# Native float32 products for the first six weight slots of layer 0, and the rotary tables computed after the first GLA

## The chip, the cores and the metric

The kernel runs on one core of a Trainium2 chip. The metric is device time in microseconds (us) of one execution. The core has a matrix engine (TensorE, PE in the profile; its weight loads are listed as PEld), a vector engine (VectorE, DVE), a scalar engine (ScalarE, ACT), a general engine (GpSimd, POOL) and a queue engine (SyncE, SP) that mostly issues transfers from device memory. Each engine runs its own fixed list of instructions in order, and waits on semaphores for the others.

## What is computed

Two layers of a streaming-encoder trunk on 256 tokens of width 1024, everything in float32. Each layer normalises its input, shifts and scales it by values computed from a conditioning vector c (adaLN), multiplies it by one wide input matrix, feeds three token mixers (attention with rotary keys, RWKV-7, gated linear attention or GLA), and merges them.

```python
cos, sin = _rope_tables(positions)
c_act = jax.nn.silu(c)
for l in range(DEPTH):                                  # 2 layers
    mod = c_act @ ada_w[l] + ada_b[l]                   # 1024 -> 3 x 1024
    shift, scale, gate = jnp.split(mod, 3, axis=-1)
    h = _rms_norm(x, norm_pre[l]) * (1 + scale[:, None, :]) + shift[:, None, :]
    p = h @ w_in[l]
    ...
    o_mla = _mla_branch(m_cq, m_ckv, m_kr, m_z, cos, sin, ...)
    o_rwkv = _rwkv7_branch(r_streams, r_z, ...)
    o_gla = _gla_branch(g_q, g_k, g_v, g_l, g_z, ...)
    merged = (sigmoid(gate_a) * o_mla + sigmoid(gate_b) * o_rwkv + sigmoid(gate_c) * o_gla)
    y = merged @ w_out[l]
    x = x + gate[:, None, :] * _rms_norm(y, norm_post[l])
```

## The kernel before

Activations lie transposed: 128 partitions of features, 8 feature blocks (`KD`), 256 tokens. The input matrix is cut in **slots** of 256 output columns; a slot is two transfers of 512 KB (128x1024 each) and makes one 2x256-column PSUM bank, by 8 blocks x 2 halves = 16 products of 128x128 weights by 128x256 tokens.

A product of full float32 precision is made of three products in the type float32r: weights and activations are each split into a rounded part `hi` and a rest `lo`, and `hi*hhi + hi*hlo + lo*hhi` is summed. For the weights this is done in `weights` (L333 to L347): the transfer into `wr`, the copy to `hi` on ACT (L344), the subtraction to `lo` on DVE or POOL (L345). The activations are split by `split` (L388 to L392) into `hhi` and `hlo`, once, and kept for the layer. `dense` (L358) and `dense_tok` (L371) run the products. `wr`, `hi` and `lo` rotate through four buffers each.

**The head** of the program, `start` (L268 to L320), makes layer 0's normed input and the first six slots (lora0, rk000, rk001, rr000, rr001, rv000). It loads x (L275), squares it on ACT, sums the squares of each token on PE (`sums`, L144), and takes the root and reciprocal in `rms_row` (L397): reduce, root, reciprocal on 128x2 values, then `to_rows` (L146) and `spread` (L162) turn these into a row and copy it to all partitions by two more products. x is multiplied by it (L285). Then an order string is walked, "WaWaWaWaWaWaaa". A `W` takes up one slot: its loads and splits, and a product of zeros (L315) that opens its bank. An `a` takes up one feature block k: `ada_part` (L254) loads two 512 KB tiles of the adaLN matrix and reduces each with c in one DVE instruction (L263, scalar_tensor_tensor, STT below), `ada_in` (L322) makes shift and scale, ACT applies them (L303), `split` makes `hhi` and `hlo`, and the products of block k with the slots so far follow (`mm`, L288 to L295, products at L293). In four of the six slots POOL makes `lo`. 

`rope_tables` (L172 to L213), 34 POOL instructions on 128x256 tiles and two sines on ACT, stands ahead of `start` in the program.

**Behind the head** come, for layer 0: the rest of the RWKV slots and the GLA gates (`pg`, L800, which reads the 32 KB tile `gw`), GLA's slots gq, gk, gv, `rw_prep` for half of the heads, `rw_chain(0)` (L562), `gla`, `rw_prep` and `rw_chain` for the other half, attention, and the output. In `rw_chain` a matrix `Bb` is loaded, POOL computes a triangular inverse `Xb` in 31 dependent pairs (L607 to `tm`, L610 to `Xb`), the result goes out and back by a transfer (`Xs`), and then a loop over chunks starts with the product `u` (L692).

A planner with its own model of times orders each engine's list at build time; the program text decides only what depends on what, and which pools and rotations a tile uses.

Of the kernel before, what the change touches and what calls it, by code (L numbers as in the profile page):

```python
# [10 lines left out]
F32 = mybir.dt.float32  # L11
# [65 lines left out]
def trunk(  # L77
# [94 lines left out]
    def rope_tables():  # L172
        with tc.tile_pool(name="rope", bufs=1, reuse_waits="tile") as rp:
            posi = rp.tile([P, T], I32, name="posi")
            nc.sync.dma_start(posi, pos.partition_broadcast(P))
            ang = rp.tile([P, T], F32, name="ang")
            G.tensor_copy(ang, posi)
            G.tensor_scalar(ang, ang, ifreq, None, ALU.mult)
            turn = rp.tile([P, T], F32, name="turn")
            pieces, inv2pi = _turn_pieces()  # L180

            def wrap(t):
                r = rp.tile([P, T], F32, tag="wrap", name="wrap", bufs=2)
                G.tensor_scalar(r, t, MAGIC, -MAGIC, ALU.add, ALU.add)
                G.tensor_sub(t, t, r)

            first = True
            for k, hi, lo in pieces:
                m = MAGIC * 2.0 ** k
                n = rp.tile([P, T], F32, tag="n", name="n", bufs=2)  # L190
                G.tensor_scalar(n, ang, m, -m, ALU.add, ALU.add)
                G.tensor_sub(ang, ang, n)
                a = rp.tile([P, T], F32, tag="ta", name="ta", bufs=2)
                G.tensor_scalar(a, n, 2.0 ** -k, hi, ALU.mult, ALU.mult)
                wrap(a)
                b = rp.tile([P, T], F32, tag="tb", name="tb", bufs=2)
# [7 lines left out]
            b = rp.tile([P, T], F32, tag="tb", name="tb2", bufs=2)  # L204
# [62 lines left out]

    def start(L, hl, firsts, order):  # L268
# [2 lines left out]
        hhi, hlo = hl  # L271
        zero = pp.tile([P, 1], F32, name="zero")
        G.memset(zero, 0.0)
        xn = pp.tile([P, KD, T], F32, name="xn0")
        nc.sync.dma_start(xn, xt)  # L275
        ss = ps_m.tile([P, 2, KD], F32, tag="m", name="ss0")
        for s in range(4):
            sq = pp.tile([P, 2, T], F32, tag="sq", name="sq0", bufs=2)
            A.activation(sq, xn[:, 2 * s:2 * s + 2], AF.Square)
            for i in range(2):  # L280
                sums(ss[:, :, 2 * s + i:2 * s + i + 1], sq[:, i], one_b)
        ri = rms_row(pp, ss, 1.0 / D, "0")
# [3 lines left out]
        slots, ks, left = [], [], {}  # L286

        def mm(w, ps, k):  # L288
            left[id(ps)] -= 1
            ws = slice(k * P, (k + 1) * P)  # L290
            for i, (hi, lo) in enumerate(w):
                for j, (wt, at) in enumerate(((hi, hhi), (hi, hlo), (lo, hhi))):
                    PE.matmul(  # L293
                        ps[:, i].rearrange("p (a b) -> p a b", a=2), wt[:, ws], at[:, :, k],
                        start=False, stop=i == 1 and j == 2 and left[id(ps)] == 0)  # L295

        for what in order:
            if what == "a":
                k = len(ks)
                ada_part(L, 0, (k,), pp)  # L300
                ada_in(L, k, k + 1)
                hT = pp.tile([P, T], F32, tag="hT0", name="hT0", bufs=3)
                A.activation(hT, xn[:, k], AF.Identity, scale=L.s1[:, k:k + 1], bias=L.mod[:, k:k + 1])  # L303
                split(hhi[:, :, k], hlo[:, :, k], hT.rearrange("p (a b) -> p a b", a=2))
                ks.append(k)
                for w, ps in slots:
                    mm(w, ps, k)
            else:
                n, src, pool, tag = firsts[len(slots)]
                j = len(slots)  # L310
                w = weights(src, n, pool=None if j < 2 else pp, sub=G if j in (1, 3, 4, 5) else V)
                ps = pool.tile([P, 2, T], F32, tag=tag, name=f"ps_{n}")
                left[id(ps)] = KD
                early[n] = ps
                PE.matmul(  # L315
                    ps.rearrange("p a b -> p (a b)"), zero.broadcast_to([P, P]), zero.broadcast_to([P, 512]),
                    start=True, stop=False)
                slots.append((w, ps))
# [821 lines left out]
    rw = ctx.enter_context(tc.tile_pool(name="rw", bufs=1))  # L1140
    for l in range(DEPTH):
        h = halves_of(hl)
# [14 lines left out]
        with tc.tile_pool(name=f"rc{l}0", bufs=1, reuse_waits="tile") as rc:  # L1157
# [142 lines left out]
```

## Time and profile before

| | us |
| --- | --- |
| timed runs, median of three | 1174.64 (1173.78 to 1175.44) |
| the profiled execution, its own time | 1172.76 |
| its span in the trace | 1171.0 |
| PE busy, share of the span | 1091.8 (93%) |
| PEld / DVE / ACT / POOL busy | 85% / 68% / 49% / 40% |

The profile was taken of one execution; its 1172.76 us lie 1.88 us below the median of the timed runs. PE is busy most of the time, but its busy share is lowest at the start: the tenths of the first three fortieths (29 us each) read 5, 8, 9 in the page's second part, and the granted TensorE clock in the same slices reads 7, 7, 9 tenths of full speed. Times in the trace count from the start of the span. A PE row's duration covers the whole passage of one instruction; back-to-back products overlap, so that the distance between two starts, not the duration, is what one costs.

### The profile page before, as it was taken

How to read it: one execution, taken by the hardware profiler on the slowest of the kernel's cores; microseconds unless marked ns; L12 is line 12 of the kernel's file. 1: busy time of each engine (PE TensorE's matmuls, PEld its weight loads, DVE VectorE, ACT ScalarE, POOL GpSimd, SP SyncE). 2: the span in 40 equal slices, each digit the busy share in tenths (PEclk: the TensorE clock that was granted, in tenths of full speed). 3: DMA queues.
4: the chain of work that ended last, by engine and by line, in shares of the span. 5: the costliest groups of instructions: out<-in, count | busy, mean ns of one | idle time of the engine just before them, and what ended most of it. 6: DMA issues, size and time to landing. Idle time of an engine off the chain costs nothing.

```text
span 1171.0 us, 25069 instructions
## 1 busy us (share of the span) xinstructions
PE 1091.8 (93%) x10293; PEld 997.3 (85%) x10293; DVE 791.7 (68%) x1204; ACT 576.9 (49%) x982; POOL 467.2 (40%) x617
## 2 busy tenths in 40 slices
PE   5899988899999699999989999899999979999997
PEld 3788888798898588899989888889899968789997
DVE  5968955666887666667665694385587666657763
ACT  4357334445456343445556833364383635346452
POOL 7954638425426833203100635541073753311210
PEclk7799998999999899999999999899999989999999
DMA  9665654654466454446654255334434543244761
GB/s 362 211 197 174 164 170 127 193 185 152 130 217 193 145 158 95 131 136 214 224 181 152 89 162 151 113 108 140 143 117 145 181 129 93 86 123 139 247 206 45
DMA packets 70068, 185.15 MB, mean 158 GB/s; under 512 B 24609, under 2 KB 25121, under 8 KB 69825
## 3 DMA queue, kind: packets, MB, share of 16 engines
q1 hardware_dynamic: 48304, 173.37, 47.6%
q10 hardware_dynamic: 21648, 10.18, 3.3%
q8 instruction: 81, 1.33, 0.4%
q14 instruction: 35, 0.28, 0.1%
HBM read 179.32 MB, written 4.20 MB: 157 GB/s over the span
## 4 chain that ended last, share of the span: by engine, by line
PE 60%; POOL 15%; DMA 10%; DVE 6%; ACT 4%; issue 4%; ACTq 1%; SPq 0%; DVEq 0%; POOLq 0%
PE ps_gt L358 10%; PE ps_wo L358 9%; POOL tm L607 6%; POOL Xb L610 5%; PE ps_rz L358 4%; PE ps_rv L358 4%; PE y L371 3%; PE ps_mz L358 2%; PE ps_gq L358 2%; DMA adaw<-in_ada_dram 2%; DMA wr_wout<-in_wout_dram 2%; PE ps_cq L358 2%; DMA Bb<-bd 2%; PE ps_rr L358 2%; DMA Xs<-xd 1%
## 5 line engine op out<-in xcount | busy, mean ns | idle before, releaser
L358 PE MATMUL ps_gt<-hhi,lo_gt 128*128 128x256 f32 x384 | 109.6, 286 | 0.0
L358 PE MATMUL ps_gt<-hhi,hi_gt 128*128 128x256 f32 x384 | 109.5, 285 | 0.0
L358 PE MATMUL ps_gt<-hlo,hi_gt 128*128 128x256 f32 x384 | 109.1, 284 | 0.0
L345 DVE TENSOR_TENSOR lo_gt<-wr_gt,hi_gt 128x1024 fp32r<-128x1024 f32 x48 | 61.9, 1291 | 42.2 <-ACT hi_gt L344 41.9
L345 DVE TENSOR_TENSOR lo_wo<-wr_wo,hi_wo 128x1024 fp32r<-128x1024 f32 x48 | 67.2, 1400 | 33.3 <-ACT hi_wo L344 33.0
L263 DVE SCALAR_TENSOR_TENSOR adaw<-adaw,cb 128x1024 f32<-128x1024 f32 x48 | 66.5, 1388 | 25.1 <-DMA adaw<-in_ada_dram 25.0
L607 POOL TENSOR_TENSOR tm<-Xb,Bb 128x126 f32<-128x126 f32 (+22 forms) x124 | 68.0, 548 | 30.3 <-DMA Bb<-bd 21.2
L344 ACT CAST hi_gt<-wr_gt 128x1024 fp32r<-128x1024 f32 x48 | 50.3, 1049 | 53.4 <-PE ps_gt L358 20.1
L358 PEld LDWEIGHTS ps_gt<-hhi,lo_gt 128*128 128x128 f32 x384 | 73.5, 191 | 0.8
L358 PEld LDWEIGHTS ps_gt<-hhi,hi_gt 128*128 128x128 f32 x384 | 73.6, 192 | 0.6 <-issue 0.2
L358 PEld LDWEIGHTS ps_gt<-hlo,hi_gt 128*128 128x128 f32 x384 | 73.5, 191 | 0.5
L344 ACT CAST hi_wo<-wr_wo 128x1024 fp32r<-128x1024 f32 x48 | 50.3, 1049 | 47.0 <-PE ps_wo L358 22.2
L785 POOL TENSOR_TENSOR merged<-merged,tg 128x512 f32<-128x512 f32 x14 | 24.6, 1760 | 116.1 <-DVE tg L784 92.8
L712 POOL TENSOR_TENSOR gst<-ST,GC 64x256 f32<-64x256 f32 x48 | 34.8, 725 | 76.3 <-DVE ST L716 62.7
L610 POOL TENSOR_TENSOR Xb<-Xb,tm 128x126 f32<-128x126 f32 (+22 forms) x124 | 61.6, 496 | 9.1
L643 POOL COPY bks<-vs 128x128 f32<-128x128 f32 x32 | 13.7, 429 | 123.6 <-PE ptok L650 106.5
L654 ACT COPY vals<-ptok 32x128 f32<-32x128 f32 x128 | 32.8, 256 | 51.8 <-PE ptok L650 32.1
L696 DVE COPY vals<-u 32x128 f32<-32x128 f32 x128 | 36.5, 286 | 10.7 <-PE u L692 8.9
L1037 POOL TENSOR_SCALAR pr<-pr,sm 128x128 f32<-128x128 f32 (+1 forms) x32 | 28.7, 911 | 27.6 <-DVE sm L1035 27.3
L371 PE MATMUL ps_gv<-hi_gv,hhi 128*128 128x256 f32 x128 | 37.3, 295 | 2.5 <-ACT hi_gv L344 1.4
L358 PE MATMUL ps_gz<-hlo,hi_gz 128*128 128x256 f32 x128 | 38.4, 300 | 0.0
L371 PE MATMUL ps_gv<-hi_gv,hlo 128*128 128x256 f32 x128 | 37.2, 292 | 0.9 <-DVE hlo L392 0.9
(500 smaller groups left out, 4333.7 us busy)
## 6 DMA issues: line engine op xcount, KB each, us to landing
adaw<-in_ada_dram SPq DMA_DIRECT2D x48, 512.0 KB, 4.3
wr_gt<-in_win_dram SPq DMA_DIRECT2D x48, 512.0 KB, 3.8
wr_wo<-in_wo_dram SPq DMA_DIRECT2D x48, 512.0 KB, 4.1
wr_rk<-in_win_dram SPq DMA_DIRECT2D x16, 512.0 KB, 4.2
wr_rr<-in_win_dram SPq DMA_DIRECT2D x16, 512.0 KB, 4.8
wr_rv<-in_win_dram SPq DMA_DIRECT2D x16, 512.0 KB, 3.8
wr_gv<-in_win_dram SPq DMA_DIRECT2D x16, 512.0 KB, 4.6
wr_gz<-in_win_dram SPq DMA_DIRECT2D x16, 512.0 KB, 4.3
```

The lines of the kernel that those rows point to most:

```text
L263: V.scalar_tensor_tensor(w, w, 0.5, cb, ALU.mult, ALU.mult, accum_out=L.mod[:, ADA_ORDER[2 * s + i]:ADA_ORDER[2 * s + i] + 1],)
L344: A.copy(hi, wr)
L345: (sub or V).tensor_sub(lo, wr, hi.bitcast(F32))
L358: PE.matmul(ps if len(a.shape) == 2 else ps.rearrange("p (a b) -> p a b", a=2), wt[:, at + k * P:at + (k + 1) * P], a, start=i == 0, stop= ...
L371: PE.matmul(ps, a[:, st * P:(st + 1) * P] if len(a.shape) == 2 else a[:, st], wt[:, k * n % CHUNK:k * n % CHUNK + n], start=i == 0, stop=i ...
L607: G.tensor_mul(tv, Xb[:, 0:nr, m:m + 1].broadcast_to([P, nr, w]), Bb[:, m:m + 1, m + 1:32].broadcast_to([P, nr, w]))
L610: G.tensor_add(Xb[:, 0:nr, m + 1:32], Xb[:, 0:nr, m + 1:32], tv)
L654: A.copy(vals[ch % 2][rows(g2, 1 - gh), :, gh, g2], pt[32 * g:32 * g + 32, 2].rearrange("p (q v) -> p q v", q=2))
L696: V.tensor_copy(val[rows(g2, gh), :, gh, g2], u[rows(g2, gh)])
L712: G.tensor_mul(gst[chan(qi)], ST[chan(qi), :, qi], R.GC[chan(qi), :, ch:ch + 1].broadcast_to([64, 4, 64]))
L785: (V if b == 2 and s == 3 else G).tensor_add(m, m, tg)
L1037: G.tensor_scalar(pr[:, ks], pr[:, ks], sm[:, 4 + qt:5 + qt], None, ALU.mult)
```

## The change

In `start`, the weights of the six first slots are loaded as plain float32 tiles `w` and multiplied as float32: 2 products for each block and slot instead of 6, nothing split in the weights. The activations are modulated in place in `xn`, and are still split into `hhi` and `hlo`, since everything behind the head reads those. The sum of squares is one PE product of a matrix of ones with each of the eight squared blocks, which leaves the sum of each token on every partition at once; the root and the reciprocal are then taken on 128x256 values. x comes in two transfers. The zero products of all six banks come first, and the order string begins with an `a`. The adaLN tiles have 8 buffers instead of 6. `rope_tables` is called after GLA's pools close in layer 0, with one buffer instead of two for each of its four temporaries. Lines of the changed kernel lie 7 or 8 lower than the same lines before (L358 is L365, L607 is L614).

```diff
     def rope_tables():
...
-                r = rp.tile([P, T], F32, tag="wrap", name="wrap", bufs=2)
+                r = rp.tile([P, T], F32, tag="wrap", name="wrap")
...
-                    w = pool.tile([P, D], F32, tag="adaw", name=f"adaw{l}_{s}", bufs=6)
+                    w = pool.tile([P, D], F32, tag="adaw", name=f"adaw{l}_{s}", bufs=8)
...
+        ones = pp.tile([P, P], F32, name="ones")
+        G.memset(ones, 1.0)
         xn = pp.tile([P, KD, T], F32, name="xn0")
-        nc.sync.dma_start(xn, xt)
-        ss = ps_m.tile([P, 2, KD], F32, tag="m", name="ss0")
+        for s in range(2):
+            nc.sync.dma_start(xn[:, 4 * s:4 * s + 4], xt[:, 4 * s:4 * s + 4])
+        banks = []
+        for n, src, pool, tag in firsts:
+            ps = pool.tile([P, 2, T], F32, tag=tag, name=f"ps_{n}")
+            PE.matmul(
+                ps.rearrange("p a b -> p (a b)"), zero.broadcast_to([P, P]), zero.broadcast_to([P, 512]),
+                start=True, stop=False)
+            banks.append(ps)
+        ss = ps_m.tile([P, T], F32, tag="m", name="ss0")
         for s in range(4):
             sq = pp.tile([P, 2, T], F32, tag="sq", name="sq0", bufs=2)
             A.activation(sq, xn[:, 2 * s:2 * s + 2], AF.Square)
             for i in range(2):
-                sums(ss[:, :, 2 * s + i:2 * s + i + 1], sq[:, i], one_b)
-        ri = rms_row(pp, ss, 1.0 / D, "0")
+                PE.matmul(ss, ones, sq[:, i], start=s + i == 0, stop=s + i == 4)
+        ri = pp.tile([P, T], F32, name="ri0")
+        A.activation(ri, ss, AF.Sqrt, scale=1.0 / D, bias=eps6)
+        V.reciprocal(ri, ri)
...
         def mm(w, ps, k):
-            for i, (hi, lo) in enumerate(w):
-                for j, (wt, at) in enumerate(((hi, hhi), (hi, hlo), (lo, hhi))):
-                    PE.matmul(
-                        ps[:, i].rearrange("p (a b) -> p a b", a=2), wt[:, ws], at[:, :, k],
-                        start=False, stop=i == 1 and j == 2 and left[id(ps)] == 0)
+            for i in range(2):
+                PE.matmul(
+                    ps[:, i], w[:, i, k * P:(k + 1) * P], xn[:, k],
+                    start=False, stop=i == 1 and k == KD - 1)
...
-                hT = pp.tile([P, T], F32, tag="hT0", name="hT0", bufs=3)
-                A.activation(hT, xn[:, k], AF.Identity, scale=L.s1[:, k:k + 1], bias=L.mod[:, k:k + 1])
-                split(hhi[:, :, k], hlo[:, :, k], hT.rearrange("p (a b) -> p a b", a=2))
+                A.activation(xn[:, k], xn[:, k], AF.Identity, scale=L.s1[:, k:k + 1], bias=L.mod[:, k:k + 1])
...
-                w = weights(src, n, pool=None if j < 2 else pp, sub=G if j in (1, 3, 4, 5) else V)
+                w = pp.tile([P, 2, CHUNK], F32, name=f"w_{n}")
+                for i in range(2):
+                    nc.sync.dma_start(w[:, i], src[:, i * CHUNK:(i + 1) * CHUNK])
...
+        for k in range(KD):
+            split(hhi[:, :, k], hlo[:, :, k], xn[:, k].rearrange("p (a b) -> p a b", a=2))
...
-        rope_tables()
         start(L, hl, (
...
-        ), "WaWaWaWaWaWaaa")
+        ), "aWaWaWaWaWaWaa")
...
             gla(L, l, h, gates, merged, gp)
             glap.close()
+            if l == 0:
+                rope_tables()
```

On DVE at the start of the head, from the first reduction of an adaLN tile (`adaw`, two tiles for each block) to the scaling of x (`xn`), there stood before:

```order
L263 SCALAR_TENSOR_TENSOR adaw_0_227,mod_94<-adaw_0_227,cb 128x1024
L400 TENSOR_REDUCE rr_195<-ss_170 128x2
L263 SCALAR_TENSOR_TENSOR adaw_0_230,mod_94<-adaw_0_230,cb 128x1024
L324 TENSOR_TENSOR mod_94<-mod_94,par_92 128x1
L402 RECIPROCAL rr_195<-rr_195 128x2
L325 TENSOR_TENSOR mod_94<-mod_94,par_92 128x1
L149 CAST hl_199<-rr_195 128x2
L326 SCALAR_TENSOR_TENSOR s_0_96<-mod_94,par_92 128x1
L150 TENSOR_TENSOR hl_199<-rr_195,hl_199 128x2
L263 SCALAR_TENSOR_TENSOR adaw_1_266,mod_94<-adaw_1_266,cb 128x1024
L285 TENSOR_TENSOR xn_168<-xn_168,ri_207 128x512 x4
```

and now:

```order
L263 SCALAR_TENSOR_TENSOR adaw_0_149,mod_94<-adaw_0_149,cb 128x1024
L331 TENSOR_TENSOR mod_94<-mod_94,par_92 128x1
L263 SCALAR_TENSOR_TENSOR adaw_0_152,mod_94<-adaw_0_152,cb 128x1024
L332 TENSOR_TENSOR mod_94<-mod_94,par_92 128x1
L333 SCALAR_TENSOR_TENSOR s_0_96<-mod_94,par_92 128x1
L296 RECIPROCAL ri_142<-ri_142 128x256
L263 SCALAR_TENSOR_TENSOR adaw_1_164,mod_94<-adaw_1_164,cb 128x1024
L263 SCALAR_TENSOR_TENSOR adaw_1_167,mod_94<-adaw_1_167,cb 128x1024
L299 TENSOR_TENSOR xn_110<-xn_110,ri_142 128x512 x4
```

The reduction, the split of the 128x2 reciprocals and the subtractions for `lo` are gone; a reciprocal of 128x256 has come in, and both adaLN tiles of block 1 stand ahead of the scaling of x.

On SP, behind the head's last loads, the queue that leads to the transfer of `gw` read before:

```order
L262 DMA adaw_8_1702<-in_ada_dram 128x1024
L262 DMA adaw_8_1705<-in_ada_dram 128x1024
L343 DMA wr_gq_1710<-in_win_dram 128x1024
L343 DMA wr_gq_1716<-in_win_dram 128x1024
L343 DMA wr_gq_1772<-in_win_dram 128x1024
L343 DMA wr_gq_1778<-in_win_dram 128x1024
L262 DMA adaw_9_1832<-in_ada_dram 128x1024
L793 DMA gw_707<-in_gw_dram 16x512
```

and now:

```order
L262 DMA adaw_8_1381<-in_ada_dram 128x1024
L350 DMA wr_gq_1386<-in_win_dram 128x1024
L350 DMA wr_gq_1442<-in_win_dram 128x1024
L350 DMA wr_gq_1448<-in_win_dram 128x1024
L350 DMA wr_gk_1504<-in_win_dram 128x1024
L262 DMA adaw_9_1508<-in_ada_dram 128x1024
L262 DMA adaw_9_1511<-in_ada_dram 128x1024
L350 DMA wr_gk_1516<-in_win_dram 128x1024
L800 DMA gw_377<-in_gw_dram 16x512
```

Two tiles of the slot gk and the second tile of block 9 now stand ahead of `gw`.

On POOL, where layer 0's triangular inverse begins, there stood before:

```order
L892 TENSOR_TENSOR gsq<-gsq 128x256
L600 MEMSET Xb 128x512
L602 MEMSET Xb 64x16 x2
L607 TENSOR_TENSOR tm<-Xb,Bb 128x31
L610 TENSOR_TENSOR Xb<-Xb,tm 128x31
L607 TENSOR_TENSOR tm<-Xb,Bb 128x30
L610 TENSOR_TENSOR Xb<-Xb,tm 128x30
```

and now, with the rotary tables' instructions (temporaries `wrap`, `n`, `ta`, `tb`, `ang`, `turn`) between its pairs:

```order
L184 TENSOR_SCALAR wrap<-ta 128x256
L191 TENSOR_SCALAR n<-ang 128x256
L614 TENSOR_TENSOR tm<-Xb,Bb 128x31
L185 TENSOR_TENSOR ta<-ta,wrap 128x256
L192 TENSOR_TENSOR ang<-ang,n 128x256
L617 TENSOR_TENSOR Xb<-Xb,tm 128x31
L198 TENSOR_TENSOR ta<-ta,tb 128x256
L614 TENSOR_TENSOR tm<-Xb,Bb 128x30
L202 TENSOR_TENSOR turn<-turn,ta 128x256
L197 TENSOR_SCALAR tb<-n 128x256
L617 TENSOR_TENSOR Xb<-Xb,tm 128x30
```

Sixteen of the 34 stand ahead of the first `tm`, 18 between it and the ninth pair. In PE's list 865 products of slots stood before between the first product of gq and the first `u`; now 1005 do, the added 140 being slots of the merge gates (gt, +66) and of the output matrix (wo, +74), which came later before.

## Rows read from the trace of the kernel before

**Rows 1.** Busy time by stretch: us, PE, PEld, DVE, ACT, POOL, PEclk, DMA, GB/s.

```profile
10.00:20.00 10.00, 5.16 (x34) 4.82 (x35) 7.24 (x14) 7.65 (x10) 9.43 (x11) 0.71 1.02 410
...
14.30:41.60 27.30, 16.61 (x61) 13.04 (x62) 26.31 (x46) 11.06 (x17) 26.60 (x22) 0.50 0.98 368
...
41.60:48.40 6.80, 3.76 (x31) 3.55 (x31) 6.10 (x11) 2.79 (x4) 6.64 (x5) 1.00 0.49 174
```

**Rows 2.** Chain of waits, 76 to 92: start, us, what.

```profile
77.85 2.73 PE ps_rv L358 x23
...
80.58 3.95 DMA gw<-in_gw_dram
...
86.02 4.96 PE ps_gq L358 x29
```

**Rows 3.** Groups, 14.3 to 78: line, engine, names xcount, busy us, mean ns, idle.

```profile
L263 DVE SCALAR_TENSOR_TENSOR adaw<-adaw,cb 128x1024 f32<-128x1024 f32 x18 | 26.5, 1482 | 3.6 <-DMA adaw<-in_ada_dram 3.6
...
L392 DVE TENSOR_TENSOR hlo<-hT,hhi 128x256 fp32r<-128x256 f32 x8 | 10.9, 1365 | 4.5 <-ACT hhi L391 4.5
...
L285 DVE TENSOR_TENSOR xn<-xn,ri 128x512 f32<-128x512 f32 x4 | 2.5, 680 | 1.0 <-PE ri L162 1.0
...
L345 POOL TENSOR_TENSOR lo_rr<-wr_rr,hi_rr 128x1024 fp32r<-128x1024 f32 x4 | 11.4, 2853 | 0.0
...
L206 POOL TENSOR_TENSOR turn<-turn,tb 128x256 f32<-128x256 f32 x1 | 0.7, 732 | 0.1
...
L293 PE MATMUL ps_rr<-hhi,lo_rr 128*128 128x256 f32 x32 | 9.4, 294 | 4.7 <-POOL lo_rr L345 4.7
...
L293 PE MATMUL ps_lora<-hlo,hi_lora 128*128 128x256 f32 x16 | 5.9, 370 | 6.1 <-DVE hlo L392 6.1
```

**Rows 4.** Timeline of PE: start, us, instruction.

```profile
23.60 0.58 PE L293 MATMUL ps_lora<-hhi,hi_lora 128*128 128x256 f32 x1
...
54.24 0.29 PE L293 MATMUL ps_rr<-hhi,lo_rr 128*128 128x256 f32 x1
...
54.36 0.28 PE L293 MATMUL ps_rr<-hhi,hi_rr 128*128 128x256 f32 x1
...
409.19 1.13 PE L1016 MATMUL sc<-kn,qn 128*128 128x256 f32 x4
```

**Rows 5.** Timeline of weight loads, the zero products (L315).

```profile
6.65 0.34 PEld L315 LDWEIGHTS ps_rr<-zero 128*128 128x128 f32 x1 [0.52 <-issue]
...
7.50 0.19 PEld L315 LDWEIGHTS ps_rr<-zero 128*128 128x128 f32 x1 [0.51 <-issue]
...
7.93 0.19 PEld L315 LDWEIGHTS ps_rr<-zero 128*128 128x128 f32 x1 [0.24 <-issue]
```

**Rows 6.** Timeline of ACT: the first squares, behind the transfer of x.

```profile
10.17 1.15 ACT L279 ACTIVATE sq<-xn 128x512 f32<-128x512 f32 x2 [3.60 <-DMA xn<-in_xt_dram]
```

**Rows 7.** Groups of DVE, the first 300 us: reciprocals.

```profile
L402 DVE RECIPROCAL rr<-rr 128x2 f32<-128x2 f32 x1 | 0.2, 152 | 0.0
...
L523 DVE RECIPROCAL rn<-rn 128x16 f32<-128x16 f32 x1 | 0.2, 237 | 0.0
```

**Rows 8.** Timeline of POOL: the first and last of 34 rotary instructions.

```profile
7.72 0.40 POOL L177 CAST ang<-posi 128x256 f32<-128x256 int32 x1 [1.80 <-DMA posi<-in_pos_dram]
...
67.10 0.92 POOL L185 TENSOR_TENSOR t<-t,wrap 128x256 f32<-128x256 f32 x1
```

**Rows 9.** Busy time by stretch, behind the head; columns as in Rows 1.

```profile
106.00:125.00 19.00, 16.94 (x144) 16.77 (x143) 18.96 (x23) 11.73 (x17) 12.89 (x12) 1.00 0.46 135
...
170.00:213.00 43.00, 39.26 (x294) 37.92 (x295) 24.98 (x35) 18.76 (x24) 38.69 (x69) 0.92 0.46 145
```

**Rows 10.** Chain of waits, 158 to 224: the inverse's first step, the transfer.

```profile
169.85 1.33 POOL tm L607
...
215.66 7.04 DMA Xs<-xd
```

**Rows 11.** Timeline of PE: the first product of the chunk loop.

```profile
222.83 0.65 PE L692 MATMUL u<-zs,Xs 32*32 32x64 f32 x16 [3.80 <-DMA Xs<-xd]
```

More of the change, by code (lines that the diff above doesn't have):

```diff
@@ L189, in rope_tables @@
                 m = MAGIC * 2.0 ** k
-                n = rp.tile([P, T], F32, tag="n", name="n", bufs=2)
+                n = rp.tile([P, T], F32, tag="n", name="n")
                 G.tensor_scalar(n, ang, m, -m, ALU.add, ALU.add)
                 G.tensor_sub(ang, ang, n)
-                a = rp.tile([P, T], F32, tag="ta", name="ta", bufs=2)
+                a = rp.tile([P, T], F32, tag="ta", name="ta")
                 G.tensor_scalar(a, n, 2.0 ** -k, hi, ALU.mult, ALU.mult)
                 wrap(a)
-                b = rp.tile([P, T], F32, tag="tb", name="tb", bufs=2)
+                b = rp.tile([P, T], F32, tag="tb", name="tb")
                 G.tensor_scalar(b, n, 2.0 ** -k, lo, ALU.mult, ALU.mult)
@@ L203, in rope_tables @@
                 first = False
-            b = rp.tile([P, T], F32, tag="tb", name="tb2", bufs=2)
+            b = rp.tile([P, T], F32, tag="tb", name="tb2")
             G.tensor_scalar(b, ang, inv2pi, None, ALU.mult)
@@ L285, in start @@
             V.tensor_mul(x2, x2, ri.unsqueeze(1).broadcast_to([P, 2, T]))
-        slots, ks, left = [], [], {}
+        slots, ks = [], []
         def mm(w, ps, k):
-            left[id(ps)] -= 1
-            ws = slice(k * P, (k + 1) * P)
-            for i, (hi, lo) in enumerate(w):
-                for j, (wt, at) in enumerate(((hi, hhi), (hi, hlo), (lo, hhi))):
-                    PE.matmul(
-                        ps[:, i].rearrange("p (a b) -> p a b", a=2), wt[:, ws], at[:, :, k],
-                        start=False, stop=i == 1 and j == 2 and left[id(ps)] == 0)
+            for i in range(2):
+                PE.matmul(
+                    ps[:, i], w[:, i, k * P:(k + 1) * P], xn[:, k],
+                    start=False, stop=i == 1 and k == KD - 1)
         for what in order:
@@ L308, in start @@
             else:
-                n, src, pool, tag = firsts[len(slots)]
-                j = len(slots)
-                w = weights(src, n, pool=None if j < 2 else pp, sub=G if j in (1, 3, 4, 5) else V)
[L312 to L318, printed above, removed]
+                n, src = firsts[len(slots)][:2]
+                w = pp.tile([P, 2, CHUNK], F32, name=f"w_{n}")
+                for i in range(2):
+                    nc.sync.dma_start(w[:, i], src[:, i * CHUNK:(i + 1) * CHUNK])
+                early[n] = banks[len(slots)]
+                slots.append((w, early[n]))
                 for k in ks:
-                    mm(w, ps, k)
+                    mm(*slots[-1], k)
+        for k in range(KD):
+            split(hhi[:, :, k], hlo[:, :, k], xn[:, k].rearrange("p (a b) -> p a b", a=2))
     def ada_in(L, k0=0, k1=8):
@@ L1130, in trunk @@
     with tc.tile_pool(name="pre", bufs=1, side="right", reuse_waits="tile") as pp:
-        ct = pp.tile([P, D], F32, tag="adaw", name="ct", bufs=6)
+        ct = pp.tile([P, D], F32, tag="adaw", name="ct", bufs=8)
         A.activation(ct, cb, AF.Tanh, scale=0.5)
         V.scalar_tensor_tensor(cb, ct, 1.0, cb, ALU.add, ALU.mult)
-        rope_tables()
         start(L, hl, (
```

## The prediction

> **What bounds the kernel now.** I read the page's clock and busy tenths first (both lowest in the first 87 us), then the chain of waits, and then busy time by stretch. The chain shows where a gain must arrive: PE ends the last product of the six first slots and of rv001 at 80.58, waits 3.95 us for gw, and starts the first gq at 86.02 [rows 2]. From there on the chain is mostly PE's. So the change is worth what it moves the first gq, less what is given back later.
>
> In the head PE is not the bound. Its 288 products start 0.12 us apart when they run densely at full clock [rows 4], 34.6 us in all, but first product to gq takes 23.60 to 86.02 [rows 4, 2]. In 14.3 to 41.6 DVE is busy 26.31 us of 27.30 and POOL 26.60, PE only 16.61, and the granted clock is 0.50, which is the level of 1.2 GHz; from 41.6 it is 1.00 with PE still half idle [rows 1]. The groups name who is waited for: POOL's lo of the weights (4.7 us of PE idle time in front of one group of products, 2.85 us for each subtraction) and DVE's hlo (6.1 us in front of another) [rows 3]. DMA moves 410 GB/s at 10 to 20 [rows 1], but drops to 174 later: transfers are not what ends the head. It is the splitting: two engines full of it, and PE short of its pieces.
>
> **Start of the products.** x lands at about 10.2 [rows 6]. The time of the norm is then hidden behind adaLN: DVE has both tiles of block 1 ahead of the scaling of x. Behind x stand six transfers of 512 KB up to that second tile; 512 KB at 410 GB/s is 1.28 us, so it lands at 10.2 + 7.7 = 17.9, some 0.3 earlier since the positions no longer go ahead. Then one STT (1.48 us mean, and it has less company now, so I take 1.2), the first of four scalings (0.68) [rows 3], and the modulation on ACT (about 0.6): first product at 20.0, against 23.60. The 128x256 reciprocal isn't in the trace. From 152 ns for 2 and 237 for 16 elements [rows 7] it is 6 ns an element, an estimate of 1.7 us; were it a multiple of that, it would start behind block 0's STTs at about 16 and end by 18 anyway, so it costs between 0 and 2 us, and I take 0; a gain is excluded, since nothing waits for the norm earlier than for the STTs. The eight products with the matrix of ones, 0.43 to 0.86 each, follow ACT's squares as these land, 11 to 15, and the sixth zero product stands ahead of x's landing; both lie in PE's idle time, and would cost what they last if x came earlier. The two transfers of x, the eighth adaLN buffer and the single buffers of the rotary temporaries (one engine uses them, in its order) I cost at nothing.
>
> **Products.** A float32 product appears as two records. The zero products, of 512 columns, show them 0.85 apart and later 0.43 apart, doubled speed [rows 5]; half the columns make 0.43 for a product of 256 at the faster level and 0.86 at the slower. The upper bound is the attention's products of 256 columns, four records in 1.13 us, 0.28 each and 0.57 a product [rows 4]. 96 products are 41.3 us by the first, 54 by the second. I take the first, since it is a distance of starts; the second counts whole passages, which overlap. So PE does 6.7 us more work than 34.6, and in exchange waits for nothing but x's blocks: the twelve copies of ACT and twelve subtractions (eight on POOL, 2.85 us [rows 3]) are gone, and rv001's and gq's loads no longer queue behind the rotation of their buffers.
>
> True float32 in four passes is what the Trainium skill states (FP8 and Floating Point Precision, TensorE Precision Notes). By it a product would be 4 x 0.12 = 0.48 us, an estimate, and the six slots 46.1: native products are then dearer on PE than three pieces by a third, which speaks against this edit, and the head would gain 4.8 us less. The zero products' spacing gives 0.43, lower than this, and the trace decides.
>
> **Clock.** At the start PE is sparse; I assume that the slower level holds for 20 to 28, as after the sparse stretches before. 8 us there do 4 us of full-speed work: +3.8. Gaps: 0.5. The head ends at 20 + 41.3 + 3.8 + 0.5 = 65.6, against 80.58 - 2.73 = 77.85 [rows 2]: 12.2 us earlier. DVE doesn't stop it: 16 STTs at 1.2 to 1.48, 19 to 24 us, the scalings 2.5, the reciprocal 1.7 and eight hlo, 0.4 to 1.4 each [rows 3], make 27 to 39 from about 13 on, and block 7 is ready at 50 to 55. Nor do the transfers: some 16 MB at 410 GB/s are 40 us.
>
> **Behind the head.** rv001's 48 products at 0.12 end at 71.4 (they need hhi and hlo, whose copies now come without haste). gw has two gk tiles and one adaLN tile more ahead of it in SP's queue, each waiting for the release of a buffer; it stands to land at about 71. With 1.1 us of pg and a gap of 1.4 the first gq starts at 74.0: **12.0 us earlier**. Queued behind gw are the LoRA tile and gk's; they wait for nothing that is not needed later.
>
> **The rotary tables.** 34 POOL instructions leave the head (7.72 to 67.10 [rows 8]; there they are off PE's path but beside DVE's work). Sixteen fill POOL's idle time ahead of the inverse; 18 stand between its first steps. Priced by the shortest add (0.73) [rows 3] and the last (0.92) [rows 8] they take 18 x 0.83 = 14.9; by the mean of all 34 in the head, 37.2 us together or 1.09 each, 19.7. I take the first, for an engine that works alone. The inverse before: its first step at 169.85, its last at about 212.7, Xs after 7.04 us of transfer at 222.7, PE waiting 3.80 for it [rows 10, 11]. Now: first step 12 to 14 earlier, at about 156 to 158, plus 43 and 14.9, end at 214 to 216, Xs at 224 to 226. So POOL gives the gain back on its own path. PE doesn't notice much, because 140 more products of later slots stand ahead of u, 16.8 us by 0.12: it reaches u at 219.03 - 14 (head, and the shorter stretch behind it) + 16.8 = 222, and waits 2 to 4 where it waited 3.80. These 140 products would have come later, so they are paid already. Sum at u: 16.8 ahead in work, 1 to 3 later by the clock: 14 to 15, less one or two for slots of wo that no longer fill gaps further on. **Net -13**: 1172.76 - 13 = 1159.8 for a profiled execution, 1161 to 1162 with the 1.88 by which the median stands above it. I forecast 1161. Layer 2's PE list is unchanged.
>
> **Rivals.** *The rotary instructions cost their price of the head* (19.7 with the sines' round trip on top): POOL is busy 38.69 of 43.00 in the inverse and DVE 24.98 [rows 9], so they meet there too. u is then reached at 229 to 230, PE waits 7 to 8 instead of 3.8, 4 to 6 of the gain go: 1167. For it: hlo takes 1365 ns on the mean in the head, as much as an STT of four times its size [rows 3], so engines do slow each other there. Against: DVE is busy 58% in the inverse, 96% in the head. The Trainium skill names such a cause (GPSIMD Engine Reference, Specifications): POOL shares its SBUF interfaces with DVE, and contends with DVE instructions that read two SBUF inputs, as hlo's and the STTs do; by it the dear price would come wherever the two meet.
>
> *The gain stops behind the head.* In 106 to 125 DVE is busy 18.96 of 19.00 [rows 9]. If its work there is paced by the arrival of adaLN and weights and not by PE, PE waits for the lo tiles and all but 0 to 6 us are lost: 1170. Against: the clock is 1.00 and PE 16.94 of 19.00, 2 us of slack at most in that stretch, and DVE's STTs of the head come 10 us earlier.
>
> *Slower: the clock.* Native products may leave PE with waits between blocks, so that it stays at 0.50 as in 14.3 to 41.6 [rows 1]. All 96 at 0.86 are 82.6 us; the head ends at 102.6, 24.7 later than now: 1199. It decides from where the slower level lasts past 52 (each us of it costs half a us; 12 us of gain are eaten in 24). Against: before, the clock rose at 41.6 with PE 55% busy.
>
> *More.* PE never waits, gw is early, POOL and DVE no longer slow each other and the inverse shortens: -20, 1154.
>
> **How the numbers follow.** Forecast (1155 to 1165, the ends of the reciprocal, of gw and of the 1 to 4 us at u) 0.60; rotary price 0.15 (1167); gain stops 0.11 (1170, between 1167 and 1174); clock 0.07 (1199); more 0.07 (1154). The dear bound of a product, 0.57, adds 12.9 us to the head and alone would turn the forecast into the third case; it is in that chance. A range of 1153 to 1170 leaves out the clock and half of the third. A difference within 0.2%, 2.35 us, is about what a measurement of this kernel can't tell from no change: 0.05, from the third case, whose rest is faster. Faster 0.60 + 0.15 + 0.06 + 0.07 = 0.88, same 0.05, slower 0.07.
>
> **What would show it.** In the profile after: zero products and native pairs 0.215 apart per record; the clock at 1.00 from about 28; last native product at 64 to 68; gq at 73 to 76; the inverse's first step at 156 to 158 with a span of 57 to 60; the wait ahead of u of 2 to 4. The forecast is wrong if native records stand over 0.25 apart, if the clock stays at 0.50 past 40, if gw lands after 75, or if PE waits over 6 us for Xs.

## The result: slower by 1.1%

The changed kernel takes 1185.67 us (median of 5 runs, 1182.45 to 1192.77) against 1175.44 for the kernel before on the same chip (5 runs): a ratio of 1.0109, 95% interval 1.0083 to 1.0135. In a later set of runs the ratio was 1.0106 (1.0072 to 1.0140). Forecast were 1161 us and a gain. The profiled execution has a span of 1183.9 us (before 1171.0).

### The head: nearly as forecast, up to one wait

The timeline of PE in the changed kernel shows the first product, the last two blocks of products, and what follows them:

```profile
20.51 2.08 PE L304 MATMUL ps_lora<-xn,w_lora 128*128 128x256 f32 x4 [7.38 <-ACT xn L313]
...
61.25 1.03 PE L304 MATMUL ps_lora<-xn,w_lora 128*128 128x256 f32 x4
62.11 1.89 PE L304 MATMUL ps_rk<-xn,w_rk 128*128 128x256 f32 x8
63.84 1.89 PE L304 MATMUL ps_rr<-xn,w_rr 128*128 128x256 f32 x8
65.56 1.03 PE L304 MATMUL ps_rv<-xn,w_rv 128*128 128x256 f32 x4
66.24 0.47 PE L365 MATMUL ps_rv<-hhi,hi_rv 128*128 128x256 f32 x1
...
74.16 2.07 PE L807 MATMUL pg<-krgl,gw 16*128 16x256 f32 x4 [3.62 <-DMA gw<-in_gw_dram]
76.16 0.58 PE L365 MATMUL ps_rv<-hhi,hi_rv 128*128 128x256 f32 x1
...
79.52 0.41 PE L365 MATMUL ps_gq<-hhi,hi_gq 128*128 128x256 f32 x1
79.74 0.41 PE L365 MATMUL ps_gq<-hlo,hi_gq 128*128 128x256 f32 x1
```

The first product starts at 20.51 (before 23.60 [rows 4], forecast 20.0), four records take 0.86 from start to start, so a product costs 0.43, and the native products end at 66.2 (before 77.85 [rows 2], forecast 65.6). But `pg` then waits 3.62 us for `gw`, which lands at 74.1, and after that wait products start 0.21 to 0.22 apart. The first gq starts at 79.5, 6.3 earlier than before (85.86 in the same view) instead of 12. Before, the same view shows a shorter wait there:

```profile
84.58 1.13 PE L800 MATMUL pg<-krgl,gw 16*128 16x256 f32 x4 [1.10 <-DMA gw<-in_gw_dram]
...
85.86 0.30 PE L358 MATMUL ps_gq<-hhi,hi_gq 128*128 128x256 f32 x1
```

The 3.95 us beside `gw` in [rows 2] are the transfer's own time, from its issue at 80.58 to its landing at 84.54; PE went on with rv001 until 83.48 and waited 1.10.

The engines that the old head waited for are free, as the groups of DVE in the first 70 us show (compare [rows 3]):

```profile
L263 DVE SCALAR_TENSOR_TENSOR adaw<-adaw,cb 128x1024 f32<-128x1024 f32 x20 | 24.1, 1217 | 18.7 <-DMA adaw<-in_ada_dram 18.7
L399 DVE TENSOR_TENSOR hlo<-xn,hhi 128x256 fp32r<-128x256 f32 x8 | 3.4, 420 | 2.2 <-ACT hhi L398 2.2
...
L296 DVE RECIPROCAL ri<-ri 128x256 f32<-128x256 f32 x1 | 1.7, 1746 | 0.0
```

An hlo takes 420 ns where it took 1365, an STT 1217 where it took 1482, and DVE now waits 18.7 us for transfers.

### The inverse: 65 us instead of 43

POOL's timeline in the changed kernel, from the rotary tables' start to the end of the inverse (34 rotary instructions from the first row here to the row at 188.98; 62 steps of the inverse from 162.59 to 227.47):

```profile
143.74 0.86 POOL L177 CAST ang<-posi 128x256 f32<-128x256 int32 x1 [4.88 <-DMA posi<-in_pos_dram]
...
161.55 1.07 POOL L191 TENSOR_SCALAR n<-ang 128x256 f32<-128x256 f32 x1
162.59 0.24 POOL L614 TENSOR_TENSOR tm<-Xb,Bb 128x31 f32<-128x31 f32 x1
162.78 0.73 POOL L185 TENSOR_TENSOR ta<-ta,wrap 128x256 f32<-128x256 f32 x1
163.47 0.73 POOL L192 TENSOR_TENSOR ang<-ang,n 128x256 f32<-128x256 f32 x1
164.16 0.25 POOL L617 TENSOR_TENSOR Xb<-Xb,tm 128x31 f32<-128x31 f32 x1
...
184.32 1.93 POOL L209 TENSOR_SCALAR sinT<-sinT,cs 128x256 f32<-128x256 f32 x1
186.22 1.86 POOL L184 TENSOR_SCALAR wrap<-t 128x256 f32<-128x256 f32 x1
188.05 0.96 POOL L617 TENSOR_TENSOR Xb<-Xb,tm 128x100 f32<-128x100 f32 x1
188.98 0.73 POOL L185 TENSOR_TENSOR t<-t,wrap 128x256 f32<-128x256 f32 x1
...
227.24 0.23 POOL L617 TENSOR_TENSOR Xb<-Xb,tm 128x16 f32<-128x16 f32 x1
```

The positions' transfer, once the third transfer on SP's queue, now lands at 143.7, POOL waits 4.88 for it, and the sixteen instructions ahead of the inverse push its first step to 162.59, 2 us behind the landing of `Bb` (its second half is issued at 152.03 and lands 8.5 later, at 160.5). The 18 instructions inside last 17.6 us. First step before: 169.85 [rows 10]; so it starts 7.3 earlier and is 22 longer. Beside the 17.6, the inverse's own 62 steps take 2.9 us more (35.9 for 33.0), and instructions of the GLA output (`og`) inside it 2.6 more (6.5 for 3.9). The chain of waits goes on with

```profile
227.50 2.04 DMA xd<-Xb
229.56 0.65 ACTq L623
230.24 6.82 DMA Xs<-xd
237.06 0.14 issue
237.19 0.65 PE u L699 x16
```

The first u stands at 237.19, where it stood at 222.83 [rows 11]; PE waits 7.92 for it instead of 3.80, as its timeline shows:

```profile
237.19 0.65 PE L699 MATMUL u<-zs,Xs 32*32 32x64 f32 x16 [7.92 <-DMA Xs<-xd]
```

### Where the 14 us up to the second layer arise

Busy time by stretch, columns as in [rows 1], of both kernels: from the start to the first gq, to the first u, through the first chunk loop, to the second chain's first u, through its loop, and to layer 2's first product. Before:

```profile
0.00:85.90 85.90, 65.66 (x390) 56.02 (x391) 61.94 (x96) 40.38 (x62) 66.29 (x62) 0.82 0.73 258
85.90:222.80 136.90, 120.72 (x1022) 112.42 (x1022) 97.13 (x128) 63.78 (x94) 75.61 (x104) 0.96 0.57 163
222.80:314.80 92.00, 90.07 (x1057) 79.42 (x1061) 63.24 (x111) 44.68 (x92) 33.46 (x42) 0.96 0.53 167
314.80:419.00 104.20, 93.34 (x835) 85.29 (x826) 77.15 (x119) 52.42 (x86) 57.28 (x86) 0.95 0.59 179
419.00:514.80 95.80, 95.47 (x1075) 80.81 (x1074) 62.73 (x136) 41.85 (x96) 24.95 (x37) 1.00 0.45 123
514.80:610.80 96.00, 93.81 (x807) 91.93 (x795) 69.17 (x75) 53.34 (x74) 15.69 (x9) 1.00 0.61 197
```

The changed kernel:

```profile
0.00:79.50 79.50, 65.49 (x272) 52.48 (x273) 45.39 (x96) 27.08 (x47) 8.78 (x21) 0.90 0.79 299
79.50:237.20 157.70, 139.12 (x1165) 132.23 (x1164) 104.27 (x132) 75.29 (x104) 111.58 (x137) 0.92 0.56 157
237.20:334.70 97.50, 96.08 (x1120) 85.32 (x1120) 67.26 (x116) 47.79 (x97) 43.25 (x43) 0.98 0.52 165
334.70:444.50 109.80, 93.83 (x766) 82.56 (x754) 77.19 (x127) 52.00 (x89) 53.92 (x88) 0.88 0.52 152
444.50:534.50 90.00, 89.83 (x1051) 77.08 (x1050) 58.32 (x118) 39.53 (x87) 26.81 (x35) 1.00 0.43 124
534.50:624.80 90.30, 84.92 (x704) 82.54 (x693) 62.25 (x69) 48.39 (x69) 12.63 (x7) 0.96 0.59 186
```

The first stretch is 6.4 shorter, the second 20.8 longer. Of those 20.8, PE's list accounts for 16.8 (140 more slot products at 0.12; of slots alone it has 834 there against 694 before; the 865 and 1005 given with the change count other products too; the difference is the same). But the rest of the layer does not become shorter by as much. The first loop has 47 slot products more and is 5.5 longer, the second has 8 more and is 5.8 shorter. Between the loops PE has 489 slot products instead of 581, 11 us less, and the stretch is 5.6 *longer*: PE is idle 16.0 us there (10.9 before) at a granted clock of 0.88 (0.95). The piece of it from the last u of the first loop to the second inverse's first step, before and then changed, is the clearest:

```profile
315.00:364.60 49.60, 49.60 (x531) 46.64 (x528) 39.87 (x62) 27.38 (x48) 13.77 (x19) 1.00 0.59 177
334.90:385.80 50.90, 44.76 (x435) 40.39 (x435) 38.81 (x61) 28.98 (x48) 10.72 (x16) 0.83 0.53 147
```

It has 315 slot products before and 229 in the changed kernel, 10.3 us less, and is 1.3 longer: PE, busy throughout before, is idle 6.1 us, and the clock is 0.83 instead of 1.00. The chain of waits through the piece lies on PE for 36.9 us and on DVE for 2.5 before, and on PE for 12.7 and on DVE for 22.4 after. In the last stretch the changed kernel has 460 slot products instead of 563, 12.4 us less, and gains 5.7: the clock is 0.96 instead of 1.00, and PE waits 3.08 us, until 563.06, for `rhi`, the RWKV output's first piece. Layer 2 lasts the same in both (552 to 554 us from its first product to the last).

### The profile page after: what moved, and what is told of

The parts are those of the page before. It is cut to its first block, busy times and chain, and to the rows that moved or that the text cites. A ratio compares the mean times of both kernels' runs of the same rounds, so it can differ in the third digit from the quotient of the medians.

```text
span 1183.9 us, 24792 instructions
## 1 busy us (share of the span) xinstructions
PE 1100.7 (93%) x10176; PEld 1002.1 (85%) x10176; DVE 775.4 (65%) x1197; ACT 571.2 (48%) x973; POOL 453.2 (38%) x610
## 4 chain that ended last, share of the span: by engine, by line
PE 56%; POOL 15%; DMA 11%; DVE 8%; ACT 4%; issue 4%; ACTq 1%; SPq 0%; DVEq 0%; POOLq 0%
PE ps_gt L365 9%; PE ps_wo L365 8%; POOL Xb L617 5%; POOL tm L614 5%; PE ps_rz L365 4%; PE y L378 3%; PE ps_rv L365 3%; PE ps_gv L378 2%; PE ps_gz L365 2%; PE ps_rk L365 2%; DMA wr_wout<-in_wout_dram 2%; PE ps_cq L365 2%; PE ps_rr L365 2%; PE sp L709 1%; DMA Bb<-bd 1%
## 5 line engine op out<-in xcount | busy, mean ns | idle before, releaser
L365 PE MATMUL ps_gt<-hhi,lo_gt 128*128 128x256 f32 x384 | 110.8, 288 | 0.0
L365 PE MATMUL ps_gt<-hhi,hi_gt 128*128 128x256 f32 x384 | 110.5, 288 | 0.0
L365 PE MATMUL ps_gt<-hlo,hi_gt 128*128 128x256 f32 x384 | 110.3, 287 | 0.0
L263 DVE SCALAR_TENSOR_TENSOR adaw<-adaw,cb 128x1024 f32<-128x1024 f32 x48 | 62.2, 1303 | 31.3 <-DMA adaw<-in_ada_dram 31.3
L365 PEld LDWEIGHTS ps_gt<-hhi,lo_gt 128*128 128x128 f32 x384 | 74.5, 194 | 1.1
L365 PEld LDWEIGHTS ps_gt<-hhi,hi_gt 128*128 128x128 f32 x384 | 74.9, 195 | 0.4 <-issue 0.2
L365 PEld LDWEIGHTS ps_gt<-hlo,hi_gt 128*128 128x128 f32 x384 | 74.7, 194 | 0.6 <-issue 0.2
L617 POOL TENSOR_TENSOR Xb<-Xb,tm 128x126 f32<-128x126 f32 (+22 forms) x124 | 70.0, 565 | 8.6
L351 ACT CAST hi_gt<-wr_gt 128x1024 fp32r<-128x1024 f32 x48 | 50.3, 1048 | 45.2 <-PE ps_gt L365 22.4
L614 POOL TENSOR_TENSOR tm<-Xb,Bb 128x126 f32<-128x126 f32 (+22 forms) x124 | 60.6, 488 | 23.4 <-DMA Bb<-bd 14.8
L719 POOL TENSOR_TENSOR gst<-ST,GC 64x256 f32<-64x256 f32 x48 | 38.2, 797 | 80.6 <-DVE ST L723 66.6
L522 POOL TENSOR_SCALAR k<-ks,par 128x256 f32<-128x256 f32 x16 | 23.8, 1487 | 50.7 <-DVE ks L468 50.4
L365 PE MATMUL ps_wo<-rhi,hi_wo 128*128 128x256 f32 x128 | 37.4, 293 | 3.1 <-ACT rhi L398 3.1
L365 PE MATMUL ps_wo<-ghi,hi_wo 128*128 128x256 f32 x128 | 36.6, 286 | 3.9 <-ACT ghi L398 3.7
```

Source lines behind the costliest of these rows:

```text
L263: V.scalar_tensor_tensor(w, w, 0.5, cb, ALU.mult, ALU.mult, accum_out=L.mod[:, ADA_ORDER[2 * s + i]:ADA_ORDER[2 * s + i] + 1],)
L351: A.copy(hi, wr)
L365: PE.matmul(ps if len(a.shape) == 2 else ps.rearrange("p (a b) -> p a b", a=2), wt[:, at + k * P:at + (k + 1) * P], a, start=i == 0, stop= ...
L614: G.tensor_mul(tv, Xb[:, 0:nr, m:m + 1].broadcast_to([P, nr, w]), Bb[:, m:m + 1, m + 1:32].broadcast_to([P, nr, w]))
L617: G.tensor_add(Xb[:, 0:nr, m + 1:32], Xb[:, 0:nr, m + 1:32], tv)
L719: G.tensor_mul(gst[chan(qi)], ST[chan(qi), :, qi], R.GC[chan(qi), :, ch:ch + 1].broadcast_to([64, 4, 64]))
```

## The experiments

Two theories were set against each other. **Chain theory**: the end of layer 1 follows the serial RWKV chain, and the tables inside its inverse delay it. **Head theory**: the native head costs later what it gives (products, clock), and the tables are innocent. Ratios are to the kernel before, run beside it on the same chip; "u" is layer 0's first, "layer 2" its first product (before 222.8 and 610.8). Dates come from one profile each. A second profile of the same kernel moved layer 2's start by 5.1 us (changed) and 5.9 (e5), so smaller differences of dates say little. Most of these edits also made the planner order the filling anew.

### e1_tables_first: the tables back where they stood

```diff
+        rope_tables()
         start(L, hl, (
...
             glap.close()
-            if l == 0:
-                rope_tables()
```

> The native head as in the changed kernel, with the rotary tables called ahead of start again, where they stood before. Chain theory (the end follows the first u of layer 0, and u follows POOL's inverse, into which 18 rotary instructions were put): the inverse's first step at 158 to 161, its length back at 43 to 46 us, first u at 212 to 215 against 237.2, and the whole 8 to 11 us faster than before: 1164 to 1167. Head theory (the native products or the clock cost more later than they give, the tables are innocent): 1178 to 1186, as the changed kernel.

Measured: ratio 0.9951 (0.9922 to 0.9979), some 16 thousandths below the changed kernel. The inverse runs from 161.89 to 199.0 (37 us), u starts at 208.2, layer 2 at 603.0. PE's timeline, the first u:

```profile
208.18 0.65 PE L699 MATMUL u<-zs,Xs 32*32 32x64 f32 x16 [5.49 <-DMA Xs<-xd]
```

The move of the tables makes the loss, and without it the changed head gains 0.5%. That is less than the 8 to 11 us expected: u comes 14.6 earlier and layer 2 only 7.8. With the chain early, something else sets the end.

### e2_tables_moved_only: the split head, tables behind the GLA

> The split head of before, with the rotary tables alone moved behind the first GLA. Chain theory: inverse's first step at 168 to 173, its length 60 to 66 us instead of 43, first u at 240 to 248, whole 1188 to 1196, slower than both kernels. Head theory: within 3 us of before, 1172 to 1178.

Measured: 1.0111 (1.0070 to 1.0153); inverse from 164.1 to 230.4, u at 239.2, layer 2 at 622.0. The tables' move alone costs as much as the whole change, with a first gq at 86.8. So the head's 6 to 7 us are worth nothing that can be told once u is that late, and the head theory falls.

### e6_short_inverse: the changed kernel, part of the inverse left out

```diff
-        for m in range(31):
+        for m in range(13 if (l, qp) == (0, 0) else 31):
```

> The changed kernel, with the first 13 of the 31 steps of the inverse alone in layer 0's first chain (the other 18 are left out, some 36 POOL instructions, about 22 us). Chain theory: first u about 15 to 22 earlier than 237.2, and the whole 12 to 20 faster than the changed kernel: 1165 to 1173. Head theory: the end does not depend on u's date; within 4 us of the changed kernel.

Measured: 0.9908 (0.9874 to 0.9942); u at 203.5, layer 2 at 598.7. With the tables still inside, and 36 short POOL instructions gone, the loss turns into a gain. u comes 33.7 earlier, more than the 15 to 22 expected, and layer 2 26.1 earlier. So the late inverse is enough to explain what the tables cost. It is not the only thing that changed: 645 slot products stand between the first gq and u instead of 834.

### e8_tables_behind_inverse and e11_split_head_tables_behind

The tables are made to depend on the inverse's last value, under the native and under the split head (z1 is zero):

```diff
+            G.tensor_scalar(z1, behind[:, 15, 31:32], 0.0, None, ALU.mult)
-            G.tensor_scalar(ang, ang, ifreq, None, ALU.mult)
+            G.tensor_scalar(ang, ang, ifreq, z1, ALU.mult, ALU.add)
```

> The changed kernel, with the tables made to depend on the last value of layer 0's first inverse (times zero, added to the angles), so that all their 34 POOL instructions but the first copy stand behind it. Chain theory: first gq at 79.5 as in the changed kernel, the inverse's first step at 158 to 161, length 43 to 46, first u at 205 to 212 instead of 237.2; the tables cost nothing in POOL's idle time of the chunk loop, and the whole is 6 to 12 us faster than before and 16 to 24 faster than the changed kernel. Rival (the tables cost wherever they stand on POOL, since the chunk loop needs POOL too): u as early, but the loop 8 to 15 us longer, and the whole no faster than before.

> The split head of before, tables behind the inverse as in e8_tables_behind_inverse. It prices the tables' leaving the head alone: chain theory, 2 to 6 us faster than before (first gram 3 to 5 earlier, as in e2_tables_moved_only, and the inverse as short as before). The difference to e8_tables_behind_inverse is then the native head's own worth, 4 to 8 us.

Measured: e8 0.9986 (0.9955 to 1.0018), e11 1.0074 (1.0042 to 1.0105). In e8 u is at 203.4, but the chunk loop lasts 101.9 instead of 92 (91.6 in e1, with the same 520 slot products), with POOL busy 65.29 us of it (33.46 before):

```profile
203.40:305.30 101.90, 96.67 (x1083) 84.99 (x1083) 68.13 (x112) 52.34 (x98) 65.29 (x71) 0.91 0.49 158
305.30:421.00 115.70, 100.70 (x884) 91.64 (x873) 82.44 (x125) 54.97 (x91) 61.89 (x89) 0.93 0.53 167
```

So the rival named for this run holds: the tables cost some 10 us in the loop too, whose steps use POOL. e11 is a miss for the chain theory in its simple form: u at 205.7, the second u at 408.1, both earlier than before, and yet layer 2 starts at 619.7, 8.9 later. Its PE waits 12.4 us for the second Xs at 396 with 544 slot products behind the first loop, and has 684 left for the last stretch (563 before), which lasts 110 us instead of 96. Why the planner left so much for the end was not shown; that it had laid the work out for other dates than the chip's is a guess. The native head's worth is 8.8 thousandths here, about 10 us.

### gw early: e5, e9, e10

The 32 KB of `gw` are loaded at the very start, into the tile `merged`, which is free until the merge.

```diff
+    merged0 = lay.tile([P, KD, T], F32, tag="merged", name="merged0")
+    gw0 = merged0.rearrange("p k t -> p (k t)")[:, 0:512]
+    nc.scalar.dma_start(gw0[64:80], gw2[0])
```

> As e1_tables_first, and the 32 KB tile gw is loaded at the very start into memory that is free until the merge. First gq at 72 to 74 instead of 79.5. If PE's date there paces what leads to the inverse, first u 5 to 6 earlier than in e1_tables_first and the whole 1158 to 1161; if DVE and the transfers pace that stretch, u and the whole move less than 2 us.

> As e8_tables_behind_inverse, with gw loaded at the very start. If the wait for gw (3.6 us and a fall of the clock behind it) is worth what it lasts: 3 to 6 us faster than e8_tables_behind_inverse, 10 to 16 faster than before. If later stages take it back: within 2 us of e8_tables_behind_inverse.

> The changed kernel with gw loaded at the very start. pg no longer waits 3.6 us, the clock does not fall behind it, first gq at 73 to 75. If PE's idle and slow time add up to the end wherever they lie, the whole is 3 to 7 us faster than after_again; if POOL's inverse with the tables in it still sets u, u moves as Bb does, and the whole is 0 to 3 faster and still slower than before.

> e5_tables_first_gw_early once more for its time: native head, tables ahead of it, gw early. 5 to 10 us faster than before.

> The changed kernel once more, beside the others on one chip: 8 to 14 us slower than before.

Measured: e5 0.9940 (0.9902 to 0.9978) and, again, 0.9973 (0.9952 to 0.9993); e9 0.9951 (0.9923 to 0.9978); e10 0.9993 (0.9973 to 1.0013); the changed kernel again 1.0106 (1.0072 to 1.0140). With the tables first, gw early is worth nothing that can be told from e1. Behind the inverse (e9 against e8) it is worth 3.5 thousandths, some 4 us, as expected; the 10 to 16 us against before became 6. On the changed kernel it is worth 11 thousandths, some 13 us, about twice the most that I expected. Its inverse is as long as ever (153.3 to 218.5, 65 us), u stands at 227.4, later than before, and PE waits 11.46 for it; but layer 2 starts at 604.0. Busy time by stretch of e10, from the first u to layer 2:

```profile
227.40:319.70 92.30, 92.30 (x1074) 81.06 (x1074) 65.35 (x114) 46.42 (x95) 37.84 (x43) 0.96 0.50 162
319.70:426.60 106.90, 92.84 (x788) 82.93 (x776) 74.87 (x125) 49.72 (x84) 48.96 (x87) 0.89 0.54 165
426.60:514.00 87.40, 87.33 (x1029) 74.68 (x1031) 57.10 (x119) 39.04 (x89) 24.12 (x34) 1.00 0.39 116
514.00:604.00 90.00, 87.89 (x752) 86.00 (x742) 64.37 (x71) 50.74 (x71) 14.86 (x8) 1.00 0.60 198
```

Against the changed kernel's second profile (gq at 77.6, u at 233.5, layer 2 at 619.7) u is 6.1 earlier, and every later stretch is shorter too, by 0.9 to 4.9: the first loop by 4.9, since its list has 483 slot products there and not 529, and the last one has 508 left and not 460, so that nothing waits for `rhi`. The earlier transfer changed the planner's list as well as the dates. How much of the 13 us is the earlier date and how much the other list was not separated: no run holds the list fixed and moves the date alone.

### e12_old_norm: e1 with the norm of before

> e1_tables_first with the norm of before (sums, rms_row, to_rows, spread) in place of the products with ones and the 128x256 reciprocal. If the norm lies behind the adaLN tiles, as the prediction had it, the first product stays within 0.7 us of e1_tables_first's 19.8 and the whole within 2 us; if the norm paced it, the first product comes 2 to 4 us later, and the whole up to 4.

Measured: 0.9976 (0.9952 to 1.0001), the first product at 20.73 against 19.80 in e1, layer 2 at 604.6 against 603.0. The norm by ones is worth about 1 us at the first product (19.25 to 19.80 in the three profiles with this norm and the tables first), a little more than the 0.7 expected of a hidden norm; at the end no difference to e1 can be told.

### What the runs say together

| kernel | first gq | first u | layer 2 | u to layer 2 | ratio |
| --- | --- | --- | --- | --- | --- |
| before | 85.9 | 222.8 | 610.8 | 388.0 | 1 |
| changed | 79.5 | 237.2 | 624.8 | 387.6 | 1.0109 |
| e2, tables moved only | 86.8 | 239.2 | 622.0 | 382.8 | 1.0111 |
| e10, changed, gw early | 74.3 | 227.4 | 604.0 | 376.6 | 0.9993 |
| e1, tables first | 80.3 | 208.2 | 603.0 | 394.8 | 0.9951 |
| e6, short inverse | 77.5 | 203.5 | 598.7 | 395.2 | 0.9908 |
| e8, behind inverse | 76.8 | 203.4 | 612.1 | 408.7 | 0.9986 |
| e11, split, behind | 86.9 | 205.7 | 619.7 | 414.0 | 1.0074 |

Two things bound layer 1. Where u is late (227 to 239), the stretch from it to layer 2 is 377 to 388 us, though 2118 to 2154 slot products are left for it instead of before's 2258 (388.0 us): 104 to 140 products less, 12 to 17 us at 0.12, shorten it by 0 to 11. The work that waits for u (two loops, the second inverse, the output) sets much of that length. Where u is early (203 to 208), 2307 to 2349 are left, the stretch is 395 to 414, and layer 2 does not follow u: PE's own work, its gaps and its slower clock decide, and where the list puts the filling. How much of either length is the chain's alone was not measured, since no run takes the filling away. The grid of six kernels gives the tables' move 1.1% under the split head and 1.6% under the native one, and the native head 0.5% with the tables first, 0.9% with them behind the inverse, nothing with them inside it.

## Why the prediction was wrong

- **Start of the products**: right. 20.51 for 20.0. The reciprocal took 1.75 us (estimate 1.7), ended at 17.0 and cost nothing, as bounded.
- **Products**: right. 0.43 us, from the zero products' spacing; end at 66.2 for 65.6. The Trainium skill's four passes (FP8 and Floating Point Precision, TensorE Precision Notes) would have been 0.48 by the estimate; the trace has 0.43, which is 3.6 float32r products and not four.
- **Clock in the head**: right in size. The slower level held from 15.9 to 26.1; the rival of a head at 1.2 GHz throughout did not come.
- **gw**: wrong by 3 us in its date (74.1 for 71), and wrong in what follows. I had read the wait before as 3.95 us, which is the transfer's time; PE waited 1.10. I counted a gap of 1.4 and no more; it was 3.62, fifteen of rv001's products stood behind `pg`, and the granted clock was 0.5 from 73.9 to 80.8. First gq at 79.5 for 74.0: half of the head's 12 us was gone there. The changed kernel's second profile has a wait of 1.64 and the first gq at 77.6, so part of this comes and goes.
- **The rotary price**: the 18 instructions took 17.6, between the two ends (14.9 and 19.7). What I left out stands around them: POOL's 4.88 us of waiting for the positions, by which the sixteen others ran 2 us past the landing of `Bb`, 3 us by which the inverse's own steps became longer (35.9 against 33.0 for all 62), and 2.6 us more of `og` inside it. `Bb` itself landed at 160.5, where I had the first step at 156 to 158. Inverse's end 227.5 for 214 to 216, u at 237.2 for 224 to 226.
- **The step that failed**: "These 140 products would have come later, so they are paid already." I took PE's work as the only bound, and credited 16.8 us of work ahead of u against the chain's delay. By the credit, the changed kernel's u at 237, 14.4 later, should have cost nothing. The 140 products are missing behind u (2118 slot products for 2258), and yet u to layer 2 took 387.6 us for 388.0. Where they were taken, the stretches did not shrink by as much: the piece ahead of the second inverse lost 10.3 us of products and took 50.9 for 49.6, since PE then waited for DVE and ACT and its clock fell; and the last stretch lost 12.4 and gained 5.7, with a wait for the chain's output. So the late u cost the head's gain and 14 us more, as e1 and e6 show. That the chain behind u became the bound is read from the stages and not isolated: no run makes u late with the list held fixed. Following the chain from [rows 10, 11] to the end of the layer, and asking of each stretch that loses products whether it would become shorter, was the missing step.
- **The rivals**: the rotary price had the right place and the right wait (7.92 for 7 to 8), but by it 4 to 6 us of the gain would be lost, and the result lies some 24 above the forecast, since it too counted only PE's wait at u. The slower-side rival was the clock in the head; what came, a late chain behind u, was not among them. That DVE's stretch at 106 to 125 would keep the gain did not happen: the first gram moved by 6.5 (137.7 for 144.2), about as gq did.

## What to carry to other kernels

Work that is moved off a busy stretch is paid for by the chain it lands in: before counting other work ahead of a late result as credit, follow that result to the end of the stage, and ask of each stretch that loses the other work whether it would become shorter. A serial chain on one engine (here 31 dependent pairs on POOL) is a dear place for independent instructions, even short ones; after the change the head had POOL almost idle (8.78 us of 79.5), and under the native head the old place cost least of the three tried. Where a planner orders the whole program, an early transfer of 32 KB was worth 13 us in one surrounding, 4 in another and nothing that can be told in a third, so a part is judged in more than one surrounding.

## What the runs showed of the hardware

- The wait before `pg` cost PE twice: after its 3.62 us the granted clock fell to 0.5 (the level of 1.2 GHz) for 6.9 us, and products went from 0.12 apart to 0.21. Before, after 1.10 us, it fell for 3.4 us. In e10, without that wait, no such stretch follows the head.
- DVE and POOL slow each other: hlo is 420 ns on the mean with POOL almost idle, 1365 [rows 3] in a head where POOL is busy 26.60 of 27.30 us [rows 1]. Three of those eight took 2.46 to 2.55 us, and they ran beside POOL's `lo`; the shortest took 0.41. The Trainium skill says that POOL shares its SBUF interfaces with DVE (GPSIMD Engine Reference, Specifications); the trace agrees. POOL pays as well: `wrap` took 1.07 and 2.12 us, two `Xb` steps of like size (128x110 and 128x108) 0.41 and 1.26. In the changed kernel's first inverse every step of 1.2 us or more ran for about 1 us beside a DVE instruction on a `lo` or `adaw` tile of 128x1024.
- The same kernel varies by up to 1.4% from run to run on one core (before: 1165.14 to 1181.88 in 35 runs), more than the spread of three runs had suggested.
